# A hybrid encoder layer on one core: both directions of the RWKV-7 chunk scan in joint banks, and each HGRN2 head's front asked for ahead of the outputs of the head before

## The chip, the core and the metric

One NeuronCore of a Trainium2 chip runs the whole kernel. The metric is the time of one execution in microseconds (us), the median of several runs. Engines: PE multiplies matrices (TensorE), DVE is VectorE, ACT is ScalarE, POOL is GpSimd, SP issues transfers.

## What is computed

One layer over x of 1024 tokens and 1024 channels, in fp32: RMSNorm, one projection of 10,016 columns, three branches on slices of it, each run in both directions and summed, a gated merge with an output projection, then a SwiGLU FFN and a last norm.

```
h = rmsnorm(x) @ w_in                      # columns: SSD (z, x/B/C, dt), RWKV, HGRN, gates
# RWKV-7: 8 heads of 64, state S[v,k], one step per token, forward and backward
S = S * w_t + (S @ -kk_t) (kk_t * a_t)^T + v_t k_t^T ;   y_t = S r_t
# HGRN2: 4 heads of 128, f = lb + (1 - lb) * sigmoid(.), k = 1 - f
S = diag(f_t) S + k_t v_t^T ;   o_t = S^T q_t ;   out = rmsnorm(o_fwd + o_bwd) * silu(g)
# Mamba-2 SSD: 16 heads of 64 in 2 groups, state 128
```

The kernel does the RWKV recurrence in 16 chunks of 64 tokens, with small products of 64 and 128, and the HGRN2 recurrence of each head with states per 128 tokens and, inside them, seven levels of halving blocks of decayed scores.

## The kernel before

The stages follow one another: norm and the first projections, RWKV (preparation, chunk scan, outputs), HGRN2 (line 1002 on), SSD (its loop over pairs of heads, twice eight heads), merges, FFN. Each fp32 product of the projections is three matmuls of 128 by 512 columns (high by high, high by low, low by high; L329 to L331).

**Filling matmuls.** The projections that later stages read are not a stage of their own. They are a stock of jobs (class Jobs): `J.fill(n)` asks for n steps of three matmuls, two times eight steps make a job, a half is evicted by an ACT copy (L271), and the weights are split by ACT (wh, L220) and by DVE or POOL (wl, L222). The table FILL holds how many steps are asked for at each place of a stage; SSD divides what is left. The framework's scheduler then orders each engine's instructions by its own estimates, so that filling matmuls slide to other places than the written ones, within what tiles and banks allow. Every engine then runs its list in order.

**The chunk scan** (L729 to L880). For each of 16 chunks and both directions d: c_R (L817) multiplies the incoming state by a decay part of G, ACT copies it (L818); c_U (L825) makes U, negated by DVE (L826) for one half of the partitions and by ACT (L827) for the other; c_S (L833) makes the new state, which DVE adds (L835) and multiplies into the next chunk's SV (L837, L838), POOL decays the state; c_Y (L848, L850) makes the outputs, evicted by ACT (L856) or added by DVE (L858). For the next chunk, prep_g (L802, two banks, masks on DVE L805 and L807) and prep_b (L792, ACT L793) are done between. PSUM banks: two "g" (prep_g of both directions and prep_b), two "c" (R, U, S), one "y", three "mm" (filling matmuls and one direction's Y).

**The heads** (L1002 to L1190). For each of four heads: `gates` loads and squashes the two forget gates kf, kb and the output gate; q is loaded (one buffer); DVE clamps (L1034, L1037), ACT takes logarithms (L1035), DVE sums them (scans, L1060), ACT takes E (L1061). dps and vps are score products on PE (L1075); kd (L1112 to L1114) and transposes (L1047) lead to the states (sps, L1134, summed by DVE L1137). Each of seven levels takes four subtractions (DVE L1095, POOL L1096 to L1098), one Exp (ACT L1099) and three products (DVE L1100 to L1102) into one of three "lv" buffers, then a score product whose result DVE merges into scd (L1151). POOL copies scd to sc (L1154). The outputs ops (L1168 to L1170) come in two halves from one bank; DVE and ACT evict them (L1173 to L1175), DVE takes the low part of the squares (L1176), and PE sums squares (nps: L177 for the high part, L178 for the low); ACT and DVE finish the norm (L1183 to L1185). `gates` of the next head stands ahead of the outputs, all else of it behind.

**SSD's pair loop.** POOL subtracts cumulative sums into E (L1357), DVE overwrites masked parts (L1360) and multiplies by CB (L1362), POOL adds the output part (L1381) and decays the state (L1390); PE makes st, yo and yd (L1386, L1378, L1397).

Of the kernel before, what the change touches and what calls it, by code (L numbers as in the profile page):

```python
# [383 lines left out]
def rwkv(g):  # L384
# [349 lines left out]
    with ExitStack() as es:  # L734
# [16 lines left out]
        S = []  # L751
        for d in range(2):
            t = rp.tile([P, 4, 64], F32, tag=f"S{d}", name=f"S{d}", bufs=1)
            nc.gpsimd.memset(t, 0.0)
# [112 lines left out]
        for d in range(2):  # L867
            prep_g(0, d, ld[d])
# [1255 lines left out]
```

## Time and profile before

| | us |
|---|---|
| median of 3 runs | 2473.31 |
| lowest and highest | 2464.68, 2473.44 |
| the profiled execution | 2473.65 |
| its span, first to last instruction | 2471.9 |
| PE busy in it | 2309.0 (93%) |
| DVE, POOL, ACT busy | 1633.4, 1070.9, 989.0 |

Mean granted clock of PE: 0.968 of full speed. The profile is of one execution on the one core. Its timeline gives starts and lengths; matmuls are pipelined, so a row's length runs into the next one's, and PE counts as busy where only a start-to-start time would tell that it was late. Approximate places of the stages: the scan 444 to 637 us, HGRN2 727 to 1110, SSD 1110 to 1481.

### The profile page before, as it was taken

Reading aid. Unit: us, or ns where it says so; the run is one execution under the profiler, and the core shown is the slowest. Engines: PE = TensorE matmul, PEld = TensorE weight load, DVE = VectorE, ACT = ScalarE, POOL = GpSimd, SP = SyncE. Lnnn points to the kernel's source line nnn. Section 1 sums busy time; section 2 is a strip of 40 time slices with the busy share of each in tenths; the row PEclk is TensorE's granted clock in tenths of the full one; section 3 lists DMA queues with packets and bytes.
Section 4 is the critical chain, followed back from the end, with each engine's and each line's share of the span. In section 5 each row is a group of like instructions: output and inputs, shape, how many; then the busy total and the mean of one; then the engine's idle time right before and its main releaser. Section 6 shows DMA issues by size and latency. Waiting matters only on the chain.

```text
span 2471.9 us, 37794 instructions
## 1 busy us (share of the span) xinstructions
PE 2309.0 (93%) x14785; PEld 1865.5 (75%) x14785; DVE 1633.4 (66%) x2130; ACT 989.0 (40%) x1460; POOL 1070.9 (43%) x863
## 2 busy tenths in 40 slices
PE   8998999999989889999899899999999999999985
PEld 6777778888867777778668667788788888877664
DVE  5678863456567867746666676643675455569999
ACT  6554532222454654436224236322433333344333
POOL 4433422444134543320661671421464444447885
PEclk9999999899999999999899999999899999999998
DMA  5456685654342232225635647632132222253311
GB/s 148 122 140 137 161 211 123 201 169 147 118 148 90 82 111 78 73 73 172 149 114 170 149 111 248 211 111 95 60 95 85 86 79 84 86 179 111 97 66 68
DMA packets 381215, 306.27 MB, mean 124 GB/s; under 512 B 111273, under 2 KB 323149, under 8 KB 381037
## 3 DMA queue, kind: packets, MB, share of 16 engines
q1 hardware_dynamic: 260909, 225.71, 30.8%
q10 hardware_dynamic: 119936, 77.61, 10.8%
q8 instruction: 117, 1.92, 0.3%
q0 software_dynamic: 192, 0.52, 0.1%
q14 instruction: 61, 0.50, 0.1%
HBM read 209.68 MB, written 94.11 MB: 123 GB/s over the span
## 4 chain that ended last, share of the span: by engine, by line
PE 60%; DVE 23%; POOL 5%; issue 5%; DMA 4%; ACT 3%; ACTq 0%; SPq 0%; DVEq 0%; POOLq 0%
PE mm L329 6%; PE mm L330 6%; PE mm L331 6%; PE ps L1576 6%; PE ps L1577 6%; PE ps L1578 6%; DVE acc L1915 3%; DVE ab L1793 2%; PE Gps L802 2%; PE mm L232 2%; PE mm L230 2%; PE mm L231 2%; DMA E<-cumd 2%; POOL E L1357 2%; DVE rb L1793 1%
## 5 line engine op out<-in xcount | busy, mean ns | idle before, releaser
L329 PE MATMUL mm<-x,wh 128*128 128x512 f32 (+1 forms) x1232 | 499.4, 405 | 0.5 <-ACT wh L220 0.5
L330 PE MATMUL mm<-x,wh 128*128 128x512 f32 (+1 forms) x1232 | 495.7, 402 | 0.0
L331 PE MATMUL mm<-x,wl 128*128 128x512 f32 (+1 forms) x1232 | 494.2, 401 | 0.2
L329 PEld LDWEIGHTS mm<-x,wh 128*128 128x128 f32 (+1 forms) x1232 | 234.1, 190 | 61.7 <-issue 10.6
L331 PEld LDWEIGHTS mm<-x,wl 128*128 128x128 f32 (+1 forms) x1232 | 233.9, 190 | 56.4 <-issue 6.0
L330 PEld LDWEIGHTS mm<-x,wh 128*128 128x128 f32 (+1 forms) x1232 | 234.4, 190 | 55.6 <-issue 6.8
L1578 PE MATMUL ps<-xb,rb 128*128 128x512 f32 x432 | 168.1, 389 | 0.0
L1576 PE MATMUL ps<-xb,rb 128*128 128x512 f32 x432 | 168.0, 389 | 0.0
L1577 PE MATMUL ps<-xb,rb 128*128 128x512 f32 x432 | 168.0, 389 | 0.0
L220 ACT CAST wh<-wr 128x1024 fp32r<-128x1024 f32 (+2 forms) x103 | 100.2, 973 | 118.8 <-PE mm L330 96.7
L1576 PE MATMUL ps<-rb,ab 128*128 128x512 f32 x308 | 125.8, 408 | 20.1 <-DVE acc L1915 19.1
L222 POOL TENSOR_TENSOR wl<-wr,wh 128x1024 fp32r<-128x1024 f32 x30 | 78.2, 2607 | 146.6 <-ACT wh L220 137.4
L222 DVE TENSOR_TENSOR wl<-wr,wh 128x1024 fp32r<-128x1024 f32 (+2 forms) x73 | 97.2, 1332 | 62.2 <-ACT wh L220 62.2
L1577 PE MATMUL ps<-rb,ab 128*128 128x512 f32 x308 | 122.4, 397 | 2.4 <-POOL rb L1793 2.4
L1578 PE MATMUL ps<-rb,ab 128*128 128x512 f32 x308 | 121.5, 397 | 1.5 <-DVE ab L1793 1.5
L1740 ACT CAST rb<-fs 128x512 fp32r<-128x512 f32 x85 | 52.5, 622 | 167.3 <-PE ps L1578 115.7
L271 ACT COPY st<-mm 128x512 f32<-128x512 f32 x130 | 75.6, 581 | 97.5 <-PE mm L331 77.8
L805 DVE TENSOR_TENSOR Gc<-Gps,mk 128x256 f32<-128x256 f32 x64 | 27.0, 422 | 112.0 <-PE Gps L802 59.1
L1915 DVE TENSOR_TENSOR acc<-acc,ps 128x512 f32<-128x512 f32 x148 | 94.1, 675 | 0.2 <-PE ps L1578 0.2
L1576 PEld LDWEIGHTS ps<-xb,rb 128*128 128x128 f32 x432 | 81.1, 188 | 16.9
L1578 PEld LDWEIGHTS ps<-xb,rb 128*128 128x128 f32 x432 | 81.1, 188 | 16.8
L1577 PEld LDWEIGHTS ps<-xb,rb 128*128 128x128 f32 x432 | 81.1, 188 | 16.7
(504 smaller groups left out, 5548.9 us busy)
## 6 DMA issues: line engine op xcount, KB each, us to landing
wr<-in_w_in_dram ACTq DMA_DIRECT2D x74, 512.0 KB
fr<-in_ffn_w_in_dram SPq DMA_DIRECT2D x44, 512.0 KB
E<-cumd SPq DMA_DIRECT2D x32, 512.0 KB
pg<-st ACTq DMA_DIRECT2D x48, 256.0 KB
gt<-pg SPq DMA_DIRECT2D x24, 512.0 KB
ad<-a SPq DMA_DIRECT2D x22, 512.0 KB
dr<-in_ffn_w_down_dram SPq DMA_DIRECT2D x22, 512.0 KB
ar<-ad SPq DMA_DIRECT2D x22, 512.0 KB
```

What stands on the lines that cost most here:

```text
L220: nc.scalar.copy(hi[:, :kt, :n], raw[:, :kt, :n])
L222: g.lo_eng.tensor_sub(lo[:, :kt, :n], raw[:, :kt, :n], f32(hi[:, :kt, :n]))
L271: g.nc.scalar.copy(st[:n], ps)
L329: g.nc.tensor.matmul(ps[:n], w[0][:, k, :n], xh, start=(k == 0), stop=False)
L330: g.nc.tensor.matmul(ps[:n], w[0][:, k, :n], xl, start=False, stop=False)
L331: g.nc.tensor.matmul(ps[:n], w[1][:, k, :n], xh, start=False, stop=(k == KT - 1))
L1576: nc.tensor.matmul(ps, ah, bh, start=(i == 0), stop=False)
L1577: nc.tensor.matmul(ps, ah, bl, start=False, stop=False)
L1578: nc.tensor.matmul(ps, al, bh, start=False, stop=(i == n - 1))
L1740: nc.scalar.copy(blk[:, 0], src[j])
L1793: eng.tensor_sub(blk[:, 1], s, f32(blk[:, 0]))
L1915: nc.vector.tensor_add(m[j], m[j], ps)
```

## The change

In the scan, the two directions of one chunk get joint tiles (S, SV, UV, R) and joint banks: R, U, S and Y each fill one bank of 512 columns, 32 matmuls in a row, and have one eviction (R: an ACT copy of 128x512; U: DVE 64x512 and ACT 64x512; S: a DVE sum of 128x512, two products of 64x512, one on POOL of 128x512). prep_g of the second direction takes its two banks from "mm" instead of "g". Both directions' Y use the "y" bank. PE runs the loop in written order, exempt from the scheduler.

```
-            psR = pp.tile([P, 4, 64], F32, tag="c", name="Rps", bufs=2)
-            for e, p, er in HD:
-                nc.tensor.matmul(psR[er, p], G[:, e, p, 0, :], SV[:, e, p, :], start=True, stop=True)
+            psR = bank("c", "Rps", 2)
+            for d, e, p, er in HD:
+                nc.tensor.matmul(psR[er, d, p], ld.G[d][:, e, p, 0, :], ld.SV[:, d, e, p, :], start=True, stop=True)
             nc.scalar.copy(R, psR)
...
-            nc.vector.tensor_scalar(UV[0:64, 0], psU[0:64], -1.0, None, MUL)
-            nc.scalar.mul(UV[64:128, 1], psU[64:128], -1.0)
+            nc.vector.tensor_scalar(ld.UV[0:64, :, 0], psU[0:64], -1.0, None, MUL)
+            nc.scalar.mul(ld.UV[64:128, :, 1], psU[64:128], -1.0)
...
-            pss = [pp.tile([P, 4, 2, 64], F32, tag="g", name="Gps", bufs=2) for e in range(2)]
+            pool, tag, n = (pp, "g", 2) if d == 0 else (g.mmps, "mm", 3)
...
+        order.enter_context(tc.manual_schedule(engines={PE}))
         for c in range(NS):
...
-            R = [c_R(c, d, ld[d]) for d in range(2)]
+            R = c_R(ld)
             J.fill(F[0] + (F[6] if c < 2 else 0))
             if c + 1 < NS:
-                prep_g(c + 1, 0, nx[0])
-            for d in range(2):
-                c_U(c, d, ld[d], R[d])
+                prep_g(0, nx)
+            c_U(ld, R)
             J.fill(F[1])
```

In HGRN2, a new function `front(hd)` holds gates, the q load, the clamps, the logarithms, the two scans and level 0 of a head; it is called for head 0 ahead of the loop and for head hd + 1 where `gates(hd + 1)` was called, ahead of the outputs of head hd. The buffers "t" grow from five to six, and the steps of filling at the places of a head are set anew, with the same sum per head (41 and, behind it, 26).

```
-    "hg": (7, 2, 2, 2, 2, 2, 2, 4, 6, 5, 26),
+    "hg": (4, 2, 2, 2, 2, 3, 3, 3, 10, 6, 26),
...
+        def front(hd):
+            fr = Ctx()
+            fr.kf, fr.gg = gates(hd)
+            fr.q = tl("q")
+            nc.sync.dma_start(fr.q, J.get(g.ph, hd))
+            lf = [tl("t", bufs=TB), tl("t", bufs=TB)]
+            fr.cm = [tl("cf"), tl("cb")]
...
+                nc.vector.tensor_tensor_scan(cs, on, x, 0.0, MUL, ADD)
+            fr.G = level(0, fr)
+            return fr
...
             if hd < 3:
-                nxt = gates(hd + 1)
+                nxt = front(hd + 1)
             J.fill(F[8])
```

Line numbers of the changed kernel: filling matmuls L330 to L332, wl L223; in the scan G L807 with masks L810 and L812, R L824, U L831, S L838, B L794, Y L850 and L853; in HGRN2 the norm's sums L178 (high) and L179 (low), level operations L1039 (DVE), L1040 to L1042 (POOL), products L1044 to L1046, scans L1068, merges L1162, copies of scores L1165, outputs L1179 to L1181 with evictions L1184 to L1187; in SSD yo L1389, st L1397, yd L1408.

How the order of instructions moves, at three places.

PE in the scan, one chunk. Before (a chunk in which the scheduler left no filling matmul; other chunks have up to eleven, at other places):

```order
L817 MATMUL Rps<-SVc,Gc 64x64 x16
L802 MATMUL Gps<-ARc,BKc 128x128 x8
L825 MATMUL Ups<-Rc,TTc 64x64 x16
L802 MATMUL Gps<-ARc,BKc 128x128 x8
L848 MATMUL Yps<-Gc,UVc 64x64 x2
L833 MATMUL Sps<-UVc,Btc 64x64 x16
L792 MATMUL Bps<-ident,BKc 128x128 x4
L848 MATMUL Yps<-Gc,UVc 64x64 x4
L792 MATMUL Bps<-ident,BKc 128x128 x4
L848 MATMUL Yps<-Gc,UVc 64x64 x3
L850 MATMUL Yps<-ARc,SVc 64x64 x8
L848 MATMUL Yps<-Gc,UVc 64x64 x7
```

After; all chunks but the ends have this sequence, with three filling matmuls behind U and three behind Y:

```order
L824 MATMUL Rps<-SV,Gc 64x64 x16
L807 MATMUL Gps<-ARc,BKc 128x128 x8
L831 MATMUL Ups<-Rc,TTc 64x64 x16
L330 MATMUL mm<-x_244,wh 128x512
L331 MATMUL mm<-x_245,wh 128x512
L332 MATMUL mm<-x_244,wl 128x512
L807 MATMUL Gps<-ARc,BKc 128x128 x8
L838 MATMUL Sps<-UV,Btc 64x64 x16
L794 MATMUL Bps<-ident,BKc 128x128 x8
L850 MATMUL Yps<-Gc,UV 64x64 x16
L853 MATMUL Yps<-ARc,SV 64x64 x16
L330 MATMUL mm<-x_253,wh 128x512
```

S, B and the parts of Y no longer alternate, and every chunk holds six filling matmuls.

DVE at the first boundary between heads. Before, from the first half's output product L1173 to the second half's subtraction L1176, between which stand the next head's scans and its first levels:

```order
L1037 TENSOR_SCALAR kb<-kb,lb1n,lb_4650 128x1024
L1060 SCALAR_TENSOR_TENSOR cb<-on_456,t 128x1024
L1173 SCALAR_TENSOR_TENSOR t<-ops,vcolsv_447,gg 128x512
L1095 TENSOR_TENSOR lv<-cb 128x8x64
L1095 TENSOR_TENSOR lv<-cb 128x16x32
L1095 TENSOR_TENSOR lv<-cb 128x32x16
L1185 TENSOR_TENSOR t<-t 128x512
L1100 TENSOR_TENSOR lv<-lv,q 128x1024
L1101 TENSOR_TENSOR lv<-lv,kf 128x8x64
L1102 TENSOR_TENSOR lv<-lv,kb 128x8x64
L1176 TENSOR_TENSOR t<-t 128x512
```

After, the next head's scans (L1068) and first subtractions (L1039) stand ahead of the current head's last level (L1044 to L1046 with kf 128x512):

```order
L1039 TENSOR_TENSOR lv<-cb 128x512
L1162 COPY_PREDICATED scd<-msk,vps 128x512
L1068 SCALAR_TENSOR_TENSOR cf<-on_456,t 128x1024
L1068 SCALAR_TENSOR_TENSOR cb<-on_456,t 128x1024
L1039 TENSOR_TENSOR lv<-cb 128x8x64
L1162 COPY_PREDICATED scd<-msk,vps 128x512
L1039 TENSOR_TENSOR lv<-cb 128x16x32
L1044 TENSOR_TENSOR lv<-lv,q 128x1024
L1045 TENSOR_TENSOR lv<-lv,kf 128x512
L1046 TENSOR_TENSOR lv<-lv,kb 128x512
L1045 TENSOR_TENSOR lv<-lv,kf 128x8x64
L1046 TENSOR_TENSOR lv<-lv,kb 128x8x64
```

and between the output products (L1184) and the subtractions (L1187) only the norm's product, a weight subtraction and one sum are left:

```order
L1184 SCALAR_TENSOR_TENSOR t<-ops,vcolsv_447,gg 128x512
L1187 TENSOR_TENSOR t<-t 128x512
L1100 TENSOR_TENSOR t<-kf,kb 128x1024
L223 TENSOR_TENSOR wl<-wr,wh 128x1024
L1184 SCALAR_TENSOR_TENSOR t<-ops,vcolsv_447,gg 128x512
L1196 TENSOR_TENSOR t<-t 128x512
L1187 TENSOR_TENSOR t<-t 128x512
```

On POOL, in the same place, the nine operations L1040 to L1042 of the next head's levels 0 to 2 now stand ahead of the two copies L1165; before, they came behind them. On PE, the filling matmuls between the last score product and the first output are 51 (before: 41, 40, 40), between the high and low norm sums 35, 42 and 35 (before: 44, 50 and 44, with 3 more and four transposes).

PE at the end of SSD's pair loop. Before:

```order
L1386 MATMUL st<-xw,Bt 128x512
L1397 MATMUL yd<-xt,E 128x64 x2
L1378 MATMUL yo<-S_12306,CT 128x512
L1397 MATMUL yd<-xt,E 128x64 x5
L329 MATMUL mm<-x_226,wh 128x512
L330 MATMUL mm<-x_227,wh 128x512
L331 MATMUL mm<-x_226,wl 128x512
L329 MATMUL mm<-x_235,wh 128x512
L330 MATMUL mm<-x_236,wh 128x512
L331 MATMUL mm<-x_235,wl 128x512
L329 MATMUL mm<-x_244,wh 128x512
L330 MATMUL mm<-x_245,wh 128x512
```

After, at the corresponding states (st):

```order
L331 MATMUL mm<-x_437,wh 128x512
L1408 MATMUL yd<-xt,E 128x64 x3
L1389 MATMUL yo<-S_12086,CT 128x512
L1408 MATMUL yd<-xt,E 128x64 x5
L332 MATMUL mm<-x_436,wl 128x512
L1397 MATMUL st<-xw,Bt 128x512
L1389 MATMUL yo<-S_12085,CT 128x512
L1397 MATMUL st<-xw,Bt 128x512
L1389 MATMUL yo<-S_12086,CT 128x512
L1408 MATMUL yd<-xt,E 128x64 x8
L1397 MATMUL st<-xw,Bt 128x512
```

The filling matmuls have run out there; before, 97 of them stand from here to the end of the stage.

## Rows read from the trace of the kernel before

**Rows 1.** The page's first part: busy time of each engine, its share of the span, instructions.

```profile
PE 2309.0 (93%) x14785; PEld 1865.5 (75%) x14785; DVE 1633.4 (66%) x2130; ACT 989.0 (40%) x1460; POOL 1070.9 (43%) x863
```

**Rows 2.** Stretches of the span: the second head of HGRN2 (823 to 922 us) and the end of the SSD stage (1395 to 1481 us). Columns: us, busy us (instructions) of PE, its weight loads, DVE, ACT and POOL, granted clock of PE, busy share of the DMA engines, GB/s.

```profile
823.00:922.00 99.00, 86.36 (x627) 72.17 (x626) 72.88 (x73) 55.00 (x59) 43.61 (x30) 0.93 0.27 89
1395.00:1481.00 86.00, 81.63 (x349) 57.91 (x348) 63.39 (x60) 22.49 (x26) 68.96 (x43) 0.98 0.48 118
```

**Rows 3.** Timeline of PE over one chunk of the scan without filling matmuls (start us, us, engine, line, operation, number of instructions in the row; a row's us overlap the next row's, so lengths are read from start to start).

```profile
524.31 1.15 PE L817 MATMUL Rps<-SVc,Gc 128*64 128x64 f32 x32
525.39 1.16 PE L802 MATMUL Gps<-ARc,BKc 64*128 64x128 f32 x16
526.48 1.15 PE L825 MATMUL Ups<-Rc,TTc 64*64 64x64 f32 x32
527.56 1.94 PE L802 MATMUL Gps<-ARc,BKc 64*128 64x128 f32 x16
529.43 0.39 PE L848 MATMUL Yps<-Gc,UVc 128*64 128x64 f32 x3
...
530.74 0.66 PE L792 MATMUL Bps<-ident,BKc 128*128 128x128 f32 x4
531.32 0.45 PE L848 MATMUL Yps<-Gc,UVc 128*64 128x64 f32 x8
...
534.50 0.39 PE L817 MATMUL Rps<-SVc,Gc 128*64 128x64 f32 x6
```

**Rows 4.** First row of R of the second and of the last chunk (timeline of PE); and the filling matmuls between them, one of their three lines (groups by line: line, engine, operation, names, shapes, count | busy us, mean ns | idle before).

```profile
466.31 0.28 PE L817 MATMUL Rps<-SVc,Gc 128*64 128x64 f32 x2
...
629.97 0.28 PE L817 MATMUL Rps<-SVc,Gc 128*64 128x64 f32 x2
...
L329 PE MATMUL mm<-x,wh 128*128 128x512 f32 x24 | 10.4, 434 | 0.0
```

**Rows 5.** Evictions in the scan, 466 to 637 us, by line and shape: line, engine, operation, names, shapes, count | busy us, mean ns of one | idle before, and what ended it. The last row is a DVE sum out of a full bank, of the page's fifth part (whole span).

```profile
L805 DVE TENSOR_TENSOR Gc<-Gps,mk 128x256 f32<-128x256 f32 x56 | 23.6, 422 | 53.8 <-PE Gps L802 53.1
L793 ACT COPY Btc<-Bps 128x512 f32<-128x512 f32 x28 | 16.1, 586 | 47.7 <-PE Bps L792 47.7
...
L1915 DVE TENSOR_TENSOR acc<-acc,ps 128x512 f32<-128x512 f32 x148 | 94.1, 675 | 0.2 <-PE ps L1578 0.2
```

**Rows 6.** Waits of PE in the HGRN2 stage (727 to 1110 us): what waited for what, us in total, times, longest.

```profile
PE nps L178 <- DVE t L1176: 13.8, 3, 5.2
PE tps L1047 <- DVE t L1114: 9.2, 3, 6.6
PE nps L177 <- ACT t L1175: 1.3, 2, 0.7
```

**Rows 7.** PE behind the first boundary between heads (timeline of PE), and the stretch 830 to 835 us with the columns of rows 2.

```profile
830.35 0.63 PE L330 MATMUL mm<-x,wh 128*128 128x512 f32 x1
830.77 0.63 PE L331 MATMUL mm<-x,wl 128*128 128x512 f32 x1
...
837.30 0.39 PE L330 MATMUL mm<-x,wh 128*128 128x512 f32 x1
837.53 0.39 PE L331 MATMUL mm<-x,wl 128*128 128x512 f32 x1
...
830.00:835.00 5.00, 5.00 (x13) 3.88 (x13) 5.00 (x5) 3.66 (x6) 1.96 (x1) 0.51 0.53 157
```

**Rows 8.** The same boundary on the other engines (timelines: DVE's gap before a weight subtraction, its scans and the subtraction L1176; POOL's copies of scores, and the first and last of the nine level operations with the longest form of one; a table load on ACT).

```profile
788.85 1.22 DVE L222 TENSOR_TENSOR wl<-wr,wh 128x1024 fp32r<-128x1024 f32 x1 [4.46 <-ACT wh L220]
808.85 2.28 DVE L1060 TENSOR_TENSOR_SCAN cf<-on,t 128x1024 f32<-128x1024 uint8 x1
827.32 2.38 DVE L1176 TENSOR_TENSOR t<-t 128x512 fp32r<-128x512 f32 x1
...
790.81 3.51 POOL L1154 TENSOR_SCALAR sc<-scd 64x512 f32<-64x512 f32 x2 [14.41 <-DVE scd L1151]
811.30 1.06 POOL L1096 TENSOR_TENSOR lv<-cf 128x512 f32<-128x512 f32 x1 [16.98 <-DVE cf L1060]
823.38 2.02 POOL L1097 TENSOR_TENSOR lv<-cf 128x512 f32<-128x512 f32 x1
825.37 1.48 POOL L1098 TENSOR_TENSOR lv<-cb 128x512 f32<-128x512 f32 x1
826.81 2.34 POOL L1112 TENSOR_TENSOR t<-cf 128x1024 f32<-128x1024 f32 x1
...
832.88 1.28 ACT L1183 ACT_TABLE_LOAD   x1
```

**Rows 9.** Tile kf of the second head, 870 to 900 us: its load's issue and its first use (line, engine, operation, count: duration ns min/median/max, first and last start).

```profile
L1016 SPq DMA_DIRECT2D kf<-ph x1: 320/320/320, 882.1 to 882.1; - x1
L1019 ACT ACTIVATE kf<-kf x1: 1057/1057/1057, 887.9 to 887.9; 128x1024 f32<-128x1024 f32 x1
```

**Rows 10.** One iteration over a pair in the last part of the SSD stage, 1443.44 to 1457.25 us (timelines of POOL and of DVE).

```profile
1443.44 4.21 POOL L1357 TENSOR_TENSOR E<-E,cums 128x1024 f32<-128x1024 f32 x2
...
1447.69 2.37 DVE L1360 COPY_PREDICATED E<-m,E 128x1024 f32<-128x1024 uint8 x1 [1.19 <-POOL E L1357]
1449.95 2.05 DVE L222 TENSOR_TENSOR wl<-wr,wh 128x1024 fp32r<-128x1024 f32 x1
...
1457.25 1.90 POOL L1357 TENSOR_TENSOR E<-E,cums 128x1024 f32<-128x1024 f32 x1
```

More of the change, by code (lines that the diff above doesn't have):

```diff
@@ L29 @@
 EB = 5
+TB = 6
 PE = mybir.EngineType.PE
@@ new lines, in load_early, with loads @@
+            return out
+        def loads(c, early):
+            ld = Ctx()
+            ld.AR, ld.BK, ld.TT = zip(*early)
+            ld.UV, ld.SV = (rp.tile([P, 2, 2, 4, 64], F32, tag=n, name=n) for n in ("UV", "SV"))
+            ld.G = [rp.tile([P, 2, 4, 2, 64], F32, tag=f"G{d}", name="Gc") for d in range(2)]
+            for d in range(2):
+                cc = c if d == 0 else NS - 1 - c
+                vs = Vs[cc // 2, (cc % 2) * 64:(cc % 2) * 64 + 64]
+                for e in range(2):
+                    er = slice(e * 64, e * 64 + 64)
+                    nc.gpsimd.tensor_scalar(ld.G[d][er, e, :, 0, :], ld.AR[d][er, :, 0, :], 1.0, None, MUL)
+                for t in (ld.SV, ld.UV):
+                    nc.sync.dma_start(t[64:128, d, 0], vs[:, 0])
+                    nc.sync.dma_start(t[0:64, d, 1], vs[:, 1])
+            if c == 0:
+                nc.gpsimd.memset(ld.SV[0:64, :, 0], 0.0)
+                nc.gpsimd.memset(ld.SV[64:128, :, 1], 0.0)
+            return ld
@@ new lines, in c_S @@
+        def c_S(c, ld, Bt, nxt):
+            psS = bank("c", "Sps", 2)
+            for d, e, p, er in HD:
+                nc.tensor.matmul(psS[er, d, p], Bt[d][:, p, er], ld.UV[:, d, e, p, :], start=True, stop=True)
+            pc = PC[:, :, c].unsqueeze(3).broadcast_to([P, 2, 4, 64])
+            nc.vector.tensor_add(S, S, psS)
+            nc.vector.tensor_mul(nxt.SV[0:64, :, 0], S[0:64], pc[0:64])
+            nc.vector.tensor_mul(nxt.SV[64:128, :, 1], S[64:128], pc[64:128])
+            nc.gpsimd.tensor_mul(S, S, pc)
@@ new lines, in c_Y @@
+        def c_Y(c, ld):
+            psY = bank("y", "Yps", 1)
+            for d, e, p, er in HD:
+                nc.tensor.matmul(psY[er, d, p], ld.UV[:, d, e, p, :], ld.G[d][:, e, p, 1, :],
+                                 start=(d == 0 and p == 0), stop=False)
+            for d, e, p, er in HD:
+                nc.tensor.matmul(psY[er, d, p], ld.SV[er, d, e, p, :], ld.AR[d][er, p, 1, :],
+                                 start=False, stop=(d == 1 and p == 3))
+            for d in range(2):
+                yv = Y[:, :, c, :] if d == 0 else Y[:, :, NS - 1 - c, ::-1]
+                if c < NS // 2:
+                    nc.scalar.copy(yv, psY[:, d])
+                else:
+                    nc.vector.tensor_add(yv, yv, psY[:, d])
@@ L860, in rwkv @@
         F = FILL["ch"]
-        ea = [load_early(0, d) for d in range(2)]
-        ld = [loads(0, d, ea[d]) for d in range(2)]
-        ea = [load_early(1, d) for d in range(2)]
+        ea = load_early(0)
+        ld = loads(0, ea)
+        ea = load_early(1)
         J.fill(F[4])
-        bt = [prep_b(0, d, ld[d]) for d in range(2)]
+        bt = [prep_b(d, ld) for d in range(2)]
         J.fill(F[5])
         for d in range(2):
-            prep_g(0, d, ld[d])
+            prep_g(d, ld)
+        order = ExitStack()
```

191 lines of the change are left out of this document (72 added, 119 removed).

## The prediction

> **What bounds the kernel now.** I read the busy table first, then the stretches by stage, then TensorE's (PE's) own waits, then the timeline of each place that the change touches. PE is busy for 2309.0 of 2471.9 us [rows 1]: nothing else can be the bound over the whole span, so a gain must come from PE waits, from PE time between useful matmuls, or from a better place for the filling projection matmuls. The two stretches say where to look: in the second HGRN head PE is busy 86.36 of 99 us, in the last 86 us of the SSD stage 81.63 [rows 2]. The scan shows no idle PE at all, yet its chunks hold slack, which only the start-to-start times show: R, the first G and U take 1.08, 1.09 and 1.08 us, but the second G, as large as the first, takes 1.87 (527.56 to 529.43) [rows 3]. Its two banks come from the same two as the first G, and the masks on VectorE (DVE, L805), 0.42 us each, must empty them first [rows 5].
>
> All times below are fill-equal: where the changed kernel has done more filling matmuls at a point, each counts 0.2275 us, their pitch at full clock (837.30 to 837.53) [rows 7].
>
> **1. The scan.** Both directions now share banks, PE runs in written order, and the second G has its own banks. A chunk without filling takes 10.19 us now (524.31 to 534.50) [rows 3]. Without the loss of 1.87 - 1.09 = 0.78 us at the second G, and without the changes between Y, S and B that alternate there (six, some 0.3 us by my estimate), it needs 9.1. The new order puts six filling matmuls into each chunk (1.37) and two changes to and from them (0.2): 10.65. The joint evictions are longer: R's on ScalarE (ACT) takes about 0.586, as the 512-column Bt copy L793 [rows 5]; it hides behind the 1.09 of G. U's are two in a row, on DVE about 0.675, as the 512-column sum L1915, then on ACT about 0.58 [rows 5]. The first G's four masks (0.42 each) stand ahead of U's on DVE: from R's start 2.2 + 1.6 + 0.68 + 0.58 = 5.1 us, and PE reaches S at 3.25 + 0.9 + 1.09 = 5.2. There is hardly anything to spare, so I charge 0.1: 10.75 a chunk. S's chain on DVE (sum about 0.68, two products of up to 0.8) has over 4 us of B, Y and fill in front of the next R. Fourteen chunks are 150.5 us against 163.66 now (466.31 to 629.97) with 72 filling matmuls inside (24 on each of three lines) [rows 4]; 84 afterwards. That is 13.2 + 12 x 0.2275 = 15.9. The first and last chunk, which hold the same second G, add about 3: **19 us**, ends 10 (0.6 us more of waiting in each chunk) and 25 (no charge, and less of the first chunk at a slow clock).
>
> **2. The heads.** Before, the next head's scans and its first three levels' subtractions and products stand on DVE between an output's product and the subtraction L1176 on which its norm (PE, L178) waits; PE lost 13.8 us there in three places, 1.3 us at L177 and 2.6 us of L1047's 9.2 (the other 6.6 is the first head's start, which stays) [rows 6]: 17.7. Each wait also slows what follows: after the longest, 5.2 us [rows 6], the matmuls ran 0.425 apart (830.35, 830.77) at a granted clock of 0.51 [rows 7], the lower of the two levels; eleven matmuls lost 0.2 each, 2.2 us, and three waits about 6. In the new order these waits have no cause: level 0 to 2 and the scans are done before the outputs, and 35 filling matmuls (8 us) lie before L179, whose chain (on ACT two table loads of 1.28 [rows 8] and four operations of half a row, about 0.6 each, on DVE two, about 0.7) sums to about 6.4.
>
> What is late next: the two scans, 2.28 us each [rows 8], now stand ahead of level 6's multiplications. DVE had 4.46 us idle there (788.85) [rows 8], so level 6's scores are late by 0 to 2 us; I take 1. On GpSimd (POOL) nine level operations now stand ahead of the two copies of the scores, which the outputs need. The same nine took 12.7 us of work (811.30 to 826.85, the waits for scans left out), the copies 3.5 [rows 8]. Six can run before level 6's scores end; the last three need a buffer which these scores set free. PE has 51 filling matmuls there, 11.6 us, for 3 x 1.5 + 3.5 = 8 us plus what is left of the six: 0 to 5 us late, I take 1. Six us for three heads: net **18 us**, ends 3 and 24.
>
> The next head's q load (one buffer) can start only after level 6's product. A 512-KB load issued beside two others landed in 5.8 us (882.1 to 887.9) [rows 9]; DVE then has some 12 us of work ahead of the outputs' product (the products of three levels at 0.7 to 2.06, two clamps, a weight subtraction), and PE needs that bank about 21 us after level 6's scores begin. Hidden, with about 4 us to spare.
>
> **3. What is given back.** The filling matmuls are a fixed stock: 3792 in either order. Counted in both orders, the changed kernel has done 34 more at the end of the scan and 97 more (22.1 us) at the last HGRN output; in the SSD stage they run out two and a half iterations before the end. There they are a cover, not the bound. An iteration of 13.8 us follows the chain POOL's two subtractions 4.21, DVE's predicated copy 2.37, then, each 0.7 to 1.3 us by their size, xw, state sum, L1362 and yt on DVE and two products on POOL, which ends where the next begins (1443.44 to 1457.25) [rows 10]: 12 to 12.5 us whether PE fills or not. Without filler an iteration saves the weight subtraction on DVE (2.05 in this one) [rows 10] and most of the 6 us behind the last state: 4 to 9 of 22.1. Price: **17 us**, ends 13 and 21, and 1 us for a lower clock afterwards.
>
> **Sum:** -19 - 18 + 17 + 1 = -19 from the profiled run's 2473.65 (span 2471.9; the median of the runs is 2473.31, so nothing is to be corrected): **2455 us**, 0.8% faster.
>
> **Rivals.**
> (a) *PE is the bound in SSD after all.* For it: PE is busy 81.63 of 86 us there [rows 2]. Against: that is filler, and the chain closes on itself. Then only about 7 us are lost: 2444. Chance 0.14.
> (b) *The outputs wait on POOL.* POOL and DVE hinder each other: L1176 took 2.38 us, where a sum of the same size takes 0.675 (L1915 [rows 5]), and ended 0.55 after POOL's L1112 let go (826.81 + 2.34 = 829.15, against 829.70) [rows 8]. The longest form of the level operations is 2.02 [rows 8]; if all nine take it, the copies end 5 us late, per head instead of 1: 12 us, and a slow clock behind each wait, 6. The heads then gain nothing, 2455 + 18 = 2473; between that and the forecast, 2468. Chance 0.12.
> The Trainium skill's page "SBUF — State Buffer" (Who interferes with whom) has it that a DVE operation with two SBUF inputs and a reading GpSimd operation exclude each other for whole instructions; the 829.70 above agrees, and by that rule every POOL level operation that meets a DVE product is paid in full, which is this rival.
> (c) *SSD runs bare and cold.* PE's own work there (yd, st, yo, about 7 us busy an iteration) goes at half clock when filler is gone, as it did at 830.35 [rows 7], and lengthens the chain by up to 4 us an iteration; loss 17 + 10: 2465. Chance 0.12.
> The page "TensorE: Matmul & The Clock Gate" of the Trainium skill (Part 1) calls the throttled state the default which activity lifts; by it the bare end of SSD is slow throughout, and the sum would be that of (c).
> (d) *Slower: the q load holds DVE.* Place: the first product of the next head's level 0, ahead of the current head's outputs on DVE. The new order asks for q, two gates and the input together, 2 MB; at the mean rate of this stretch, 89 GB/s [rows 2], they need 23.6 us, and the outputs' bank comes 13.5 us late in each of three heads: +40, so 2455 + 40 = 2495. It costs anything only when q needs more than 10 us, and makes the kernel slower by the bound from about 20 us on (2455 + 3 x 10.3). The 5.8 us speaks against it [rows 9]. Chance 0.08.
> (e) *The order does not do it*: scan waits move from G to S and U, and each later stage returns its gain: 2473. Chance 0.04. The forecast itself: 0.50.
>
> **How the numbers follow.** Half a per cent, 12.4 us, is about what a measurement of this kernel can tell from no change: faster is under 2461, slower over 2486. The forecast's own range is 2446 to 2464; nine tenths of it, (a), and a quarter of (b) and (c) lie under 2461: faster 0.65; the rest of these and (e): same 0.26; (d) and a little of (b): slower 0.09. The best ends together, -25 - 24 + 13, would be 2438, the worst, -10 - 3 + 21 + 1, 2483. The range leaves out (d) and the far end of the worst: 2438 to 2474.
>
> **What would show it.** Right: R to R about 10.75 us with six filling matmuls inside; no PE wait at the norms' second half (L179) on L1187; level 6's scores and the first outputs wait under 2 us; SSD's last iterations about 12 us with PE mostly idle; the SSD stage about 5 us shorter while 97 matmuls lighter. Wrong: R to R above 11.5; PE waits at the outputs on POOL's copies; DVE idle on the q load; the SSD stage as much shorter as its matmuls, or not at all.

## The result, and the profile after

| | before | after |
|---|---|---|
| median, us | 2473.28 (4 runs) | 2452.53 (4 runs) |
| lowest and highest | 2464.68, 2473.44 | 2451.22, 2458.51 |
| the profiled execution and its span | 2473.65, 2471.9 | 2453.83, 2452.1 |
| mean granted clock of PE | 0.968 | 0.963 |

The ratio is 0.9922, 95% interval 0.9907 to 0.9938: faster by 0.8%, with 2455 forecast. The busy table of after, for [rows 1]:

```profile
PE 2288.4 (93%) x14785; PEld 1847.8 (75%) x14785; DVE 1611.1 (66%) x2069; ACT 981.5 (40%) x1428; POOL 1078.3 (44%) x845
```

PE is busy for 20.6 us less, with the same number of matmuls, and the span is 19.8 us shorter. Where this comes from is seen stage by stage. In the table, each stretch of PE's timeline is compared with the same stretch of before, fill-equal as in the prediction (0.2275 us for each filling matmul done earlier); plus is a gain. The scan is counted from the first B (437.83 before, 434.25 after). Up to there PE's instructions are the same, and the 3.6 us are a difference between executions: the eleven kernels that share this part reach the first B at 434.06 to 437.83, before's trace last. The last Y and the last transpose count at their ends, the other places at their starts.

| stretch, PE | gain, us | forecast | filling matmuls ahead at its end |
|---|---|---|---|
| scan, to the last Y (636.91, 616.96) | +24.1 | +19 | 34 |
| RWKV outputs, to dps of the first head (728.54, 717.51) | -5.1 | 0 | 51 |
| first head, to its first ops (799.08, 798.98) | -3.9 | | 82 |
| from there to the last norm sum (1109.50, 1096.03) | +16.8 | | 97 |
| both stretches of the heads | +12.9 | +18 | |
| SSD, to its last transpose (1493.55, 1475.61) | -17.6 | -17 - 1 | 0 |
| rest of the span | +1.9 | 0 | |

One chunk of the scan, the timeline of PE with the columns of [rows 3]:

```profile
517.44 1.15 PE L824 MATMUL Rps<-SV,Gc 128*64 128x64 f32 x32
518.52 1.16 PE L807 MATMUL Gps<-ARc,BKc 64*128 64x128 f32 x16
519.62 1.15 PE L831 MATMUL Ups<-Rc,TTc 64*64 64x64 f32 x32
520.70 0.50 PE L330 MATMUL mm<-x,wh 128*128 128x512 f32 x1
...
521.60 1.16 PE L807 MATMUL Gps<-ARc,BKc 64*128 64x128 f32 x16
522.69 1.15 PE L838 MATMUL Sps<-UV,Btc 128*64 128x64 f32 x32
523.77 1.09 PE L794 MATMUL Bps<-ident,BKc 128*128 128x128 f32 x8
524.80 1.15 PE L850 MATMUL Yps<-Gc,UV 128*64 128x64 f32 x32
525.88 1.15 PE L853 MATMUL Yps<-ARc,SV 64*64 64x64 f32 x32
526.96 0.50 PE L330 MATMUL mm<-x,wh 128*128 128x512 f32 x1
...
527.85 0.57 PE L824 MATMUL Rps<-SV,Gc 128*64 128x64 f32 x12
```

R to R is 10.41 with six filling matmuls inside, where a chunk with none took 10.19 [rows 3]. All eight groups go at 1.03 to 1.10 from start to start, the second G too (521.60 to 522.69), and S starts with no wait. Beside it, the timelines of DVE and ACT in the same chunk (U's negation and S's sum; the evictions of R and U):

```profile
521.27 0.67 DVE L832 TENSOR_SCALAR UV<-Ups 64x512 f32<-64x512 f32 x1
...
524.35 0.67 DVE L840 TENSOR_TENSOR S<-S,Sps 128x512 f32<-128x512 f32 x1
...
518.70 0.59 ACT L825 COPY Rc<-Rps 128x512 f32<-128x512 f32 x1 [1.38 <-PE Rps L824]
521.98 0.59 ACT L833 ACTIVATE UV<-Ups 64x512 f32<-64x512 f32 x1 [2.69 <-DMA UV<-Vs]
```

The joint evictions take 0.59 (R) and 0.67 + 0.59 (U); the prediction had 0.586 and 0.675 + 0.58 from the rows nearest to them [rows 5]. U's chain ends at 521.98 + 0.59 = 522.57, 0.12 before S starts at 522.69: the "5.1 against 5.2" of the prediction.

PE's waits between RWKV's outputs and the last head, with the columns of [rows 6]:

```profile
PE vps L1108 <- DVE lv L1046: 26.1, 10, 5.2
PE tps L1085 <- DVE t L1125: 5.6, 1, 5.6
PE dps L1108 <- DVE t L1100: 4.9, 1, 4.9
PE ops L1179 <- POOL sc L1165: 1.1, 1, 1.1
```

No norm sum (L178, L179) waits any more, and of the transposes only the first head's. New against [rows 6] are dps (1.0 before in the same view) and ops; vps waited 17.5 us before. The score products that waited, the three of level 6 among them, and the first output (timeline of PE; in brackets the idle time before and who ended it):

```profile
784.94 1.15 PE L1108 MATMUL vps<-lv 128*64 128x64 f32 x32 [2.09 <-DVE lv L1046]
...
879.36 1.97 PE L1108 MATMUL vps<-lv 128*64 128x64 f32 x32 [2.09 <-DVE lv L1046]
...
975.35 1.98 PE L1108 MATMUL vps<-lv 128*64 128x64 f32 x32 [2.71 <-DVE lv L1046]
...
798.98 0.49 PE L1179 MATMUL ops<-sc,Vt 128*128 128x128 f32 x2 [1.10 <-POOL sc L1165]
```

Level 6 is 2.09, 2.09 and 2.71 late, and in two of these three heads its 32 matmuls then take 1.97 instead of 1.15: the granted clock is 0.50 from 879.4 to 881.2, the lower of the two levels, as behind the waits of before [rows 7].

The stretches of [rows 2], with its columns: the second head's 97 us, the last 86 us of SSD's pairs, and of those the last 23 (before, 1455 to 1478 had PE 22.50 busy at clock 1.00). Then POOL's first operation of three iterations there, for [rows 10]:

```profile
792.00:889.00 97.00, 88.75 (x640) 74.70 (x640) 72.05 (x75) 55.36 (x60) 43.61 (x28) 0.95 0.32 101
1376.00:1462.00 86.00, 70.84 (x263) 46.45 (x263) 67.37 (x65) 26.99 (x29) 71.31 (x43) 0.83 0.52 134
1439.00:1462.00 23.00, 18.11 (x51) 9.98 (x49) 14.85 (x18) 14.42 (x14) 17.91 (x12) 0.70 0.40 146
```

```profile
1415.89 4.20 POOL L1368 TENSOR_TENSOR E<-E,cums 128x1024 f32<-128x1024 f32 x2
...
1428.63 4.20 POOL L1368 TENSOR_TENSOR E<-E,cums 128x1024 f32<-128x1024 f32 x2
...
1441.12 4.20 POOL L1368 TENSOR_TENSOR E<-E,cums 128x1024 f32<-128x1024 f32 x2
```

The head is 2 us shorter with 2.4 us more of PE. In SSD, PE's busy time drops from 81.63 [rows 2] to 70.84 and POOL's rises from 68.96 to 71.31; the iterations are 12.74 and 12.49 long and go by their chain. PE is not "mostly idle" there, as the prediction's sign had it: it is busy 18.11 of the last 23 us, at a granted clock of 0.70. Fill-equal that stage loses 17.6; it is 4.5 us shorter (1109.50 to 1493.55 against 1096.03 to 1475.61).

### The profile page after: what moved, and what is told of

The parts are those of the page before. It is cut to its first block, busy times and chain, and to the rows that moved or that the text cites. A ratio compares the mean times of both kernels' runs of the same rounds, so it can differ in the third digit from the quotient of the medians.

```text
span 2452.1 us, 37480 instructions
## 1 busy us (share of the span) xinstructions
PE 2288.4 (93%) x14785; PEld 1847.8 (75%) x14785; DVE 1611.1 (66%) x2069; ACT 981.5 (40%) x1428; POOL 1078.3 (44%) x845
## 3 DMA queue, kind: packets, MB, share of 16 engines
q10 hardware_dynamic: 119936, 77.61, 10.8%
## 4 chain that ended last, share of the span: by engine, by line
PE 61%; DVE 23%; POOL 5%; issue 4%; DMA 3%; ACT 3%; SPq 0%; ACTq 0%; DVEq 0%; POOLq 0%
PE mm L330 7%; PE mm L331 7%; PE mm L332 7%; PE ps L1587 6%; PE ps L1589 6%; PE ps L1588 6%; DVE acc L1926 3%; DVE ab L1804 3%; PE mm L232 2%; PE mm L231 2%; PE mm L233 2%; DVE rb L1804 2%; POOL E L1368 2%; PE Gps L807 1%; DMA E<-cumd 1%
## 5 line engine op out<-in xcount | busy, mean ns | idle before, releaser
L330 PE MATMUL mm<-x,wh 128*128 128x512 f32 (+1 forms) x1232 | 500.1, 406 | 0.6 <-ACT wh L221 0.5
L332 PE MATMUL mm<-x,wl 128*128 128x512 f32 (+1 forms) x1232 | 492.3, 400 | 0.0
L330 PEld LDWEIGHTS mm<-x,wh 128*128 128x128 f32 (+1 forms) x1232 | 233.8, 190 | 61.9 <-issue 9.7
L332 PEld LDWEIGHTS mm<-x,wl 128*128 128x128 f32 (+1 forms) x1232 | 233.9, 190 | 55.1 <-issue 4.9
L223 POOL TENSOR_TENSOR wl<-wr,wh 128x1024 fp32r<-128x1024 f32 x30 | 78.9, 2630 | 133.6 <-ACT wh L221 123.1
L223 DVE TENSOR_TENSOR wl<-wr,wh 128x1024 fp32r<-128x1024 f32 (+2 forms) x73 | 98.5, 1349 | 49.6 <-ACT wh L221 49.4
L810 DVE TENSOR_TENSOR Gc<-Gps,mk 128x256 f32<-128x256 f32 x64 | 27.2, 424 | 108.2 <-PE Gps L807 62.1
L231 PE MATMUL mm<-oh,wh 128*128 128x512 f32 x224 | 88.5, 397 | 6.1 <-DVE gt L1491 4.2
L1588 PEld LDWEIGHTS ps<-xb,rb 128*128 128x128 f32 x432 | 81.1, 188 | 16.9
L1589 PEld LDWEIGHTS ps<-xb,rb 128*128 128x128 f32 x432 | 81.1, 188 | 16.8
```

The lines of the kernel that those rows point to most:

```text
L223: g.lo_eng.tensor_sub(lo[:, :kt, :n], raw[:, :kt, :n], f32(hi[:, :kt, :n]))
L231: nc.tensor.matmul(ps, whi[:, k, :n], xh, start=(k == 0), stop=False)
L330: g.nc.tensor.matmul(ps[:n], w[0][:, k, :n], xh, start=(k == 0), stop=False)
L332: g.nc.tensor.matmul(ps[:n], w[1][:, k, :n], xh, start=False, stop=(k == KT - 1))
L1588: nc.tensor.matmul(ps, ah, bl, start=False, stop=False)
L1589: nc.tensor.matmul(ps, al, bh, start=False, stop=(i == n - 1))
```

## The experiments

The runs were made in three groups, each against its own runs of the kernel before (medians 2473.15, 2474.68 and 2470.76 us). Intervals are 95%. "Change" is the kernel of the result. The columns of gains are those of the table above; "early" is the filling matmuls done ahead at the last norm sum (minus: behind), R-R the usual chunk.

| run | median, us | ratio to before | scan | to dps | to ops | to last sum | SSD | early | R-R |
|---|---|---|---|---|---|---|---|---|---|
| change | 2452.53 | 0.9922 (0.9907 to 0.9938) | +24.1 | -5.1 | -3.9 | +16.8 | -17.6 | 97 | 10.41 |
| scan_only | 2462.41 | 0.9957 (0.9942 to 0.9971) | +24.4 | -5.8 | -0.4 | -0.9 | -10.7 | 48 | 10.41 |
| heads_only | 2471.03 | 0.9991 (0.9981 to 1.0) | 0 | -0.3 | -5.0 | +14.8 | -9.5 | 47 | |
| ssd_keep | 2444.55 | 0.9884 (0.9867 to 0.99) | +28.2 | +0.1 | -4.5 | +15.0 | -8.0 | 49 | 9.50 |
| ssd_keep2 | 2441.35 | 0.9867 (0.9852 to 0.9882) | +18.0 | -1.0 | -4.8 | +15.1 | +0.6 | -3 | 9.43 |
| g_bank | 2463.30 | 0.9952 (0.9937 to 0.9967) | +16.0 | -1.6 | -3.9 | +15.9 | -15.5 | 97 | 10.74 |
| no_manual | 2503.66 | 1.0117 (1.0102 to 1.0132) | -30.7 | +1.4 | -8.8 | +18.6 | -13.8 | 84 | 10.5 to 18.1 |
| keep_h0 | 2439.28 | 0.9857 (0.984 to 0.9873) | +28.5 | +0.1 | -5.3 | +17.1 | -5.9 | 32 | 9.50 |
| r1_k1 | 2439.49 | 0.9856 (0.9841 to 0.9871) | +20.1 | -1.8 | -4.8 | +14.5 | +2.0 | -3 | 9.50 |
| order_g | 2452.99 | 0.9931 (0.9903 to 0.9958) | +20.8 | -0.5 | +0.1 | -0.8 | -0.6 | 0 | 10.70 |
| order_only | 2458.63 | 0.9949 (0.9933 to 0.9965) | +14.5 | -2.4 | -1.8 | -0.6 | +1.1 | 0 | 11.04 |
| best | 2435.64 | 0.9862 (0.9839 to 0.9884) | +23.6 | -1.8 | -4.6 | +15.9 | +2.5 | -3 | 9.50 |

**scan_only** and **heads_only**: before with the scan's part of the diff alone, and with the heads' part alone.

> The scan part of the change alone; heads, their table and buffers as before. Theory, that the terms add: the scan gains some 25 us, counted with 0.2275 us for each filling matmul done earlier, as in the trace after the change; 48 matmuls arrive in the SSD stage too early and cost half of what 97 cost, 9 us; about 2 us are lost in the RWKV outputs: 2459 us (2456 to 2464). Rival, that the first head's start cannot begin earlier and swallows the scan's gain: 10 us less gained, 2468 or more, with a long PE wait at dps or at the first transposes.

> The HGRN2 part alone (front, six t buffers, the table); scan as before. Theory: the three boundary waits and their slow clock go (17 us net of the new level waits), the first head loses about 7 us because its level 0 now stands ahead of dps and kd, and 47 filling matmuls too early in SSD cost 9: 2472 us (2467 to 2476), no change. Rival, that the first head's loss in the changed kernel came from the scan's early end and not from the front: 7 us less, 2465.

scan_only is faster by 0.4% (some 11 us) and heads_only hardly at all (0.1%), though the heads gain 10 us fill-equal in it. Each part alone does about 47 filling matmuls early and pays for them in SSD: the prices are 10.7 and 9.5, 0.2 us a matmul. In heads_only, PE's waits (columns of [rows 6]) have the new order's own marks:

```profile
PE vps L1107 <- DVE lv L1045: 25.9, 10, 5.2
...
PE ops L1178 <- POOL sc L1164: 3.6, 2, 2.5
```

vps and ops wait here as they do in the change; the wait of dps is 1.0 in the same view. So the late level 6 and the late copies belong to the heads' part. The loss ahead of dps, -5.1 in the change, belongs to the scan's part (-5.8 in scan_only, -0.3 in heads_only). The expectation had put the first head's loss of heads_only down to its own level 0; keep_h0, below, is the test of that.

**ssd_keep** takes three of the six filling matmuls out of a chunk (those behind Y), so that they are left for SSD; **ssd_keep2** takes out all six.

```
-    "ch": (0, 1, 0, 1, 0, 0, 0),
+    "ch": (0, 1, 0, 0, 0, 0, 0),      # ssd_keep
+    "ch": (0, 0, 0, 0, 0, 0, 0),      # ssd_keep2
```

(ssd_keep also lowers one entry of "hg" from 6 to 4, which leaves the order of the instructions as it is.)

> The changed kernel with the three filling matmuls behind each chunk's Y taken out of the scan's table (and two steps fewer at the output halves of a head, which moves nothing), so that 48 more are left for the SSD stage. Theory, that the end of SSD follows a chain and hides filler free of charge: half of the 17.6 us comes back, 2444 us (2440 to 2448), and PE idles less there. Rival, that PE is the bound in SSD: the 11 us saved in the scan are paid back in full, 2452.

> The changed kernel with no filling matmuls in the scan at all, 96 more left for SSD, which then has the stock that it had before the change. Theory: SSD takes as long as before and its 17.6 us come back, but without the three matmuls behind U the product S waits about 0.8 us in each of 15 chunks for U's two evictions (DVE then ACT), 12 us: 2447 us (2442 to 2450), R to R about 9.8 us. Rival, that the evictions are not near: R to R 9.1 and 2436. Rival, that PE is the bound in SSD: 2452 or more.

This is the test of the price in SSD, and it holds: with 97 and 49 matmuls early the stage loses 17.6 and 8.0, with 3 late it gains 0.6, so 0.16 to 0.18 us for each. A filling matmul in SSD thus cost 0.05 to 0.06 of its pitch of 0.2275: it was nearly free there. The stretch at the end of SSD in ssd_keep2 that answers to 1439 to 1462 of the change:

```profile
1426.00:1449.00 23.00, 22.50 (x99) 16.23 (x99) 13.78 (x16) 7.40 (x9) 15.76 (x11) 1.00 0.27 92
```

PE is busy again and at full clock. The time of ssd_keep2, 2441.35, lies just under the expected 2442 to 2450, and a chunk without filling matmuls takes 9.43, not 9.8. Yet the wait that was expected is there. S waits for ACT's half of U (from the second G to B):

```profile
526.70 1.16 PE L807 MATMUL Gps<-ARc,BKc 64*128 64x128 f32 x16
528.00 0.33 PE L838 MATMUL Sps<-UV,Btc 128*64 128x64 f32 x2
528.62 1.15 PE L838 MATMUL Sps<-UV,Btc 128*64 128x64 f32 x30 [0.30 <-ACT UV L833]
529.70 1.09 PE L794 MATMUL Bps<-ident,BKc 128*128 128x128 f32 x8
```

From G to B are 3.00 here and 2.17 in the change (521.60 to 523.77): S is 0.83 late, as the expectation's 0.8 had it. The chunk is shorter than 9.8 because the rest of it takes 8.60, not 9.0. The three behind U are almost free (9.50 against 9.43), since they stand in that wait; the three behind Y cost 0.91 (10.41 against 9.50), more than three pitches.

**g_bank** and **no_manual**: the change with the second G back in the banks of the first, and the change without the written order.

```
-            pool, tag, n = (pp, "g", 2) if d == 0 else (g.mmps, "mm", 3)
+            pool, tag, n = pp, "g", 2                                  # g_bank
-        order.enter_context(tc.manual_schedule(engines={PE}))
+                                                                       # no_manual
```

> The changed kernel with the second direction's G back in the two g banks; written order and joint evictions stay. Theory, that the second G's own banks are what the chunk gains most from: now G waits little, since three filling matmuls stand ahead of it, but B waits for its masks, 0.5 to 0.8 us in each chunk, R to R 10.9 to 11.2 us and 2459 us (2456 to 2464). Rival, that written order with filler ahead of G already covers the masks: R to R 10.4 and 2452.

> The changed kernel without the written order on PE in the scan: the scheduler places G, B, Y and filler. Theory: the alternation of kinds costs some 0.3 us in a chunk and B or G again wait for banks, 5 us in all: 2457 us (2453 to 2463). Rival, that joint banks alone give the gain: 2452 or less.

g_bank is at 0.9952 where the change is at 0.9922, and its scan gains 8.1 us less: a chunk takes 10.74, and three late chunks, which hold more filling (35, 23 and 8 matmuls), 17.76, 15.17 and 11.40. The banks are worth 0.33 in an ordinary chunk, less than the 0.78 that the prediction took off. In the trace the second G no longer waits (526.85 to 527.95); the loss sits at B, which takes 1.34 (529.06 to 530.40) instead of 1.03 and waits in its middle for a mask, as the theory had it, but for less:

```profile
529.84 0.63 PE L794 MATMUL Bps<-ident,BKc 128*128 128x128 f32 x4 [0.15 <-DVE Gc L812]
```

no_manual is slower than before, and both theories missed that. Timeline of PE in one of its chunks, and the first row of PE's waits from 440 to 660 us (columns of [rows 6]):

```profile
526.80 1.15 PE L831 MATMUL Ups<-Rc,TTc 64*64 64x64 f32 x32 [0.67 <-ACT Rc L825]
528.79 0.33 PE L838 MATMUL Sps<-UV,Btc 128*64 128x64 f32 x2 [0.84 <-DVE UV L832]
...
530.82 1.16 PE L807 MATMUL Gps<-ARc,BKc 64*128 64x128 f32 x16 [1.58 <-DMA ARc<-ARs]
```

```profile
PE Gps L807 <- DMA ARc<-ARs: 19.7, 9, 3.5
```

In this chunk R, U and S follow one another, each waiting for the whole joint eviction of the one before (0.67 for R's copy, 0.84 for U's negation), and nothing of B, G or filling stands between; G then waits for the load of its own chunk. Over the scan the loads are the larger part: 19.7 us in nine places, while the waits for evictions of R and U sum to 6.7 in eight. PE's granted clock is 0.90 over 450 to 660 us. The view's waits sum to 29 us; how the scan's loss of 30.7 splits between the waits, the clock and the filling was not itemised. What is shown: joint banks without the written order lose. That the longer waits for joint evictions are the cause is not shown; they are the smaller part, and why the loads come late stays open.

**order_only** and **order_g** ask the reverse: before, with its separate banks, given the written order alone, and then the second G's own banks too.

```
+        order = ExitStack()
+        order.enter_context(tc.manual_schedule(engines={PE}))
         for c in range(NS):
...
-            pss = [pp.tile([P, 4, 2, 64], F32, tag="g", name="Gps", bufs=2) for e in range(2)]
+            pool, tag, n = (pp, "g", 2) if d == 0 else (g.mmps, "mm", 3)     # order_g
```

> The kernel before with two edits in the scan alone: PE in written order, and the second direction's G in the mm banks. Each direction keeps its own tiles, banks and evictions; heads as before. Theory, that order and banks make the scan's gain and the joining of the directions none: R to R 10.4 to 10.6 us with six filling matmuls, some 22 us gained in the scan, nothing given back in SSD, since its stock of filler is that of before: 2451 us (2447 to 2455). Rival, that the joint banks and evictions make half of it: R to R over 11 us, 2460 or more.

> As order_g, with the second direction's G left in the g banks: written order alone. Theory: 0.35 us a chunk more than order_g, as between g_bank and the changed kernel: R to R 10.8 us, 2456 us (2451 to 2461). Rival, that with separate evictions the g banks come free later: R to R over 11.3, 2465.

order_g alone has the change's whole time (2452.99; ratio 0.9931 with the change's 0.9922 inside its interval), without joint banks and without the heads' part. The theory for it held in the time (2452.99 for 2451), not quite in the chunk (10.70 for 10.4 to 10.6). It reaches that time otherwise: 3.3 us less in the scan, no gain in the heads, and nothing early, so nothing given back. The difference to the joint banks is 0.29 a chunk (10.70, 10.41), and PE's timeline shows it at Y:

```profile
517.84 0.69 PE L850 MATMUL Yps<-Gc,UVc 128*64 128x64 f32 x16
518.46 0.68 PE L852 MATMUL Yps<-ARc,SVc 64*64 64x64 f32 x16
519.07 0.69 PE L850 MATMUL Yps<-Gc,UVc 128*64 128x64 f32 x16
519.68 0.68 PE L852 MATMUL Yps<-ARc,SVc 64*64 64x64 f32 x16
520.30 0.50 PE L329 MATMUL mm<-x,wh 128*128 128x512 f32 x1
```

Four groups of 16 take 2.46 from start to start (517.84 to 520.30), the two of 32 in the change 2.16 (524.80 to 526.96): two changes between the two kinds fewer, 0.15 for each. order_only's chunk takes 11.04 where 10.8 was expected; the 0.34 to order_g are the banks', as in g_bank.

**keep_h0** is ssd_keep with level 0 of the first head back behind the product kd. The theory: the loss between dps and the first ops (-4.5 in ssd_keep) comes from this level's early call.

```
-            fr.G = level(0, fr)
+            fr.G = level(0, fr) if hd else None
...
-            Gs = [fr.G]
+            Gs = [fr.G if hd else level(0, fr)]
```

> As ssd_keep, with level 0 of the first head alone back behind its kd, as it was before the change. Theory, that the 4.4 us which the first head loses between dps and its outputs come from its level 0 standing ahead on DVE: 3 us come back, 2441.5 us (2439 to 2444). Rival, that they come from the next head's scans ahead of level 6 and from the copies on POOL: no change, 2444.5.

The time came out as the theory said (2439.28), and the theory is wrong all the same: that stretch still loses 5.3. Timeline of PE in it, the last score product and the first output:

```profile
761.37 1.15 PE L1108 MATMUL vps<-lv 128*64 128x64 f32 x32 [1.20 <-DVE lv L1046]
...
776.58 0.79 PE L1179 MATMUL ops<-sc,Vt 128*128 128x128 f32 x2 [2.27 <-POOL sc L1165]
```

Level 6 waits 1.20 and the outputs wait 2.27 for POOL's copies: the loss is not level 0's, and the waits are those at the *next* head's front, as the rival had it (scan_only, without the heads' part, loses 0.4 there). That the time was met is luck: what keep_h0 gains on ssd_keep (0.9857 against 0.9884) lies in the trace in the later heads (+17.1 against +15.0), in SSD (-5.9 against -8.0), which had 17 matmuls more, and, 1.8 us, ahead of the scan, where the two kernels are the same.

**r1_k1** is ssd_keep with 36 filling matmuls fewer ahead of the scan, so that SSD has its old stock and three matmuls more; **best** joins it with keep_h0.

```
-    "r1": (3, 3, 3, 6, 6, 5, 5, 5, 4, 5, 4, 14, 2, 4, 17, 22, 9),
+    "r1": (3, 3, 3, 6, 6, 5, 5, 5, 4, 2, 4, 14, 2, 4, 17, 22, 9),
```

> As ssd_keep, with 36 filling matmuls fewer ahead of the scan (five steps to two at four places of the RWKV preparation), so that SSD has the stock it had before the change. Theory: SSD's 8 us of loss in ssd_keep go, and ahead of the scan 8 us of filler are saved, of which 3 come back as a wait for the scan's first loads: 2439.5 us (2436 to 2442). Rival, that those matmuls cover the loads in full: 2444.5.

> r1_k1 and keep_h0 together: the changed kernel without filler behind Y in the scan, 36 filling matmuls fewer ahead of it, and level 0 of the first head behind its kd. Theory, that the terms add: 2434.5 us (2431 to 2438). Rival, that the SSD stage or the first head's start limits both: 2439.

r1_k1 is at 0.9856 where ssd_keep was at 0.9884, and SSD loses nothing (+2.0 against -8.0). The time was met, 2439.49 for 2439.5, but the trace does not bear out its terms: the scan gains 20.1 instead of 28.2, 4.6 of the difference ahead of its first R and not the 3 expected, and the profiled execution (2442.78, the longest of four) is as long as that of ssd_keep (2442.58). So where the 5 us of the medians lie is not shown. best has the lowest median of all, 2435.64, 1.4% under before; by its ratio, 0.9862 against 0.9857 and 0.9856, it can't be told from the two that it joins, so that their gains add is not shown.

## Why the prediction was right, and where its terms were off

**The time held, the terms less so.** Forecast were gains of 19 and 18 and a loss of 18; measured are 24.1, 12.9, -5.1 that had no term, and -17.6: together 14.3. The other 5.5 of the span's 19.8 lie where nothing was edited, 3.6 ahead of the scan and 1.9 behind SSD, and no run here explains them; before's own runs lie 8.8 us apart. Three misses of 5 us, one up and two down, and this 5.5 cancel, so that the forecast's 19 is nearer to the result than its parts earn: in part luck.

**The scan** gained 24.1, not 19. The order of the steps was right: no loss at the second G, six filling matmuls inside, S just in time. Of the 24.1, 19.9 lie from the second chunk to the last (163.66 to 146.46 us with 12 more filling matmuls; forecast 15.9) and 4.1 in the first chunk, where the granted clock is 0.63 before and 0.79 after. The term that was mis-sized is the chunk, 10.75 against 10.41. Its eight groups take 8.62 from start to start, not 9.1: the six changes between groups that went were worth 0.8 (10.19 less 0.78 less 8.62) and not the 0.3 of my estimate; in Y one change costs 0.15 (order_g). The six filling matmuls cost 1.79 (0.90 behind U, 0.89 behind Y), not 1.57, and the 0.1 for U's chain was not needed. The share that I gave to the banks was too large: 0.78 was the loss in before's order, and g_bank puts the banks in the new order at 0.33. A usual chunk with six filling matmuls shows the parts best: 11.62 before, 11.04 with the written order, 10.70 with the second G's banks too, 10.41 with joint tiles. Over the whole scan, first chunk and irregular ones included, these are +14.5, +6.3 more and +3.3 more.

**What I had at nothing**: RWKV's outputs and the start of the first head lost 5.1. Of these 3.4 are on DVE ahead of dps. DVE at the start of the first head in the change (the first clamp, a scan, another clamp, and the product L1100 for which dps waits):

```profile
699.72 0.69 DVE L1059 TENSOR_SCALAR kf<-kf 128x1024 f32<-128x1024 f32 x1 [9.25 <-ACT kf L1021]
...
710.12 3.12 DVE L1068 TENSOR_TENSOR_SCAN cb<-on,t 128x1024 f32<-128x1024 uint8 x1
713.16 2.31 DVE L1059 TENSOR_SCALAR kf<-kf 128x1024 f32<-128x1024 f32 x1
715.40 2.06 DVE L1100 TENSOR_TENSOR t<-kf,kb 128x1024 f32<-128x1024 f32 x1
```

and the same rows in ssd_keep, where that stretch loses nothing:

```profile
683.76 0.69 DVE L1059 TENSOR_SCALAR kf<-kf 128x1024 f32<-128x1024 f32 x1 [8.44 <-ACT kf L1021]
...
691.85 2.28 DVE L1068 TENSOR_TENSOR_SCAN cb<-on,t 128x1024 f32<-128x1024 uint8 x1
...
696.00 2.06 DVE L1100 TENSOR_TENSOR t<-kf,kb 128x1024 f32<-128x1024 f32 x1
697.98 2.38 DVE L1059 TENSOR_SCALAR kf<-kf 128x1024 f32<-128x1024 f32 x1
```

From the first clamp to dps are 17.8 us in the change (699.72 to 717.51) and 14.35 in ssd_keep (683.76 to 698.11), as in before (714.19 to 728.54). The scheduler put a clamp of the next use (713.16, 2.31) ahead of the product, and the scan took 3.12 instead of 2.28 beside a POOL operation (L1123, 3.87 long at 711.06). scan_only has both; ssd_keep, with other filling, has neither, and nor has g_bank, with the change's own filling, which loses 1.6. Why the scheduler's estimates turn at that point, and the other 1.7 us in RWKV's outputs, stays open.

**The heads** gained 12.9, not 18. The term for the old waits was right to the tenth: all 17.7 us of waits at the norm sums and the transposes are gone. The first term that was off is "what is late next", charged at 1 us for level 6 and 1 for POOL in each head. Level 6 was late 2.09, 2.09 and 2.71, past the end of "0 to 2", and ops once by 1.10: 8.0 instead of 6. The remaining waits moved by 0.3; so waits fell by 10.0 (43.0 to 33.0, dps apart). The second is the slow clock behind the waits, where I had 6. These rows, with the columns of [rows 2], are PE's stretch from dps to the last norm sum, before and after:

```profile
728.54:1109.50 380.96, 337.90 (x2471) 282.65 (x2472) 275.44 (x278) 186.28 (x203) 163.35 (x107) 0.95 0.27 85
717.51:1096.03 378.52, 345.52 (x2517) 291.35 (x2517) 265.93 (x278) 182.64 (x201) 164.45 (x105) 0.94 0.27 86
```

The mean granted clock did not rise: level 6's own waits made PE slow again (1.97 for 1.15). So 6 us of slow clock were not saved; in what the 2.9 us beyond the waits consist no run itemises.

**SSD** gave back 17.6, forecast 17 and 1. The iteration without filling is 12.49 (forecast 12 to 12.5), and ssd_keep and ssd_keep2 show the price by taking its cause away.

**The rivals.** (a) PE as SSD's bound: no, 17.6 us were given back, not about 7. (b) The outputs wait on POOL: the place was right, the price 1.1 us in the change; heads_only had 3.6. (c) SSD cold: the clock did fall, to 0.70 in the last 23 us of the pairs, from 1.00 there before, while PE waited for the chain. It cost little: the whole stage is at 0.93 in the change and at 0.96 in ssd_keep, and the price of a matmul done early is nearly the same, 0.18 and 0.16; the difference over 97 of them is some 2 us, an estimate. By the Trainium skill's page "TensorE: Matmul & The Clock Gate" (Part 1), for which the throttled state is the default, that stretch should be slow, and the trace agrees; that the bare end is slow throughout, the last 86 us at 0.83 do not bear out, nor that it costs ten us more. (d) The q load: no engine waits for it in the heads of the change, heads_only, ssd_keep, keep_h0 or best. (e) The order does nothing: order_only alone refutes it.

## What to carry to other kernels

Filling matmuls have a price by place: ask where they are nearly free (here behind U, and in SSD's chain) and where they cost their full pitch or more (behind Y), and count how many each place has before and after a change; a stage that gets faster by emptying the stock of a later one gives most of it back. When waits are removed by asking for work earlier, price what that work now stands ahead of on each queue, and expect the slow clock to come back behind the new waits; here new waits took back 8.0 of the 17.7 us. Joint banks need the written order here: without it they were slower than what they replaced. The written order does not need them: by itself it gave 14.5 of the scan's 24.1 us, and 20.8 with separate banks for the second G.

## What the runs showed of the hardware

A change between groups of different shape on PE costs a little: in Y (128*64 and 64*64), 16 matmuls take 0.61 to 0.62 from start to start and 32 take 1.08, so cutting a group of 32 in two adds 0.15 us. Three filling matmuls between Y and R cost 0.91, not 3 x 0.2275 = 0.68. DVE's scan of 128x1024 took 3.12 beside POOL's L1123, which took 3.87 (2.34 in [rows 8]). In ssd_keep it kept its 2.28, and the POOL operation beside it (L1040 at 691.31) took 3.68, where the same operation (L1096 there) took 1.06 in [rows 8]: which of the two pays differs from case to case.
